# Grouping the bf16 and the float32r products of a split matmul on TensorE

## The chip, the cores and the metric

The kernel runs on one core of a Trainium2 chip. Times are device microseconds (us) of a whole execution. Most executions of one kernel agree within 0.3%; all timed runs used below are in the fast state or, where a kernel was run once, of unknown state with a granted TensorE clock of 0.99 or more. A run that was made once carries a time with an uncertainty of some 0.2%, so for small effects I read the trace, in which one repeated stretch of work is the same to the nanosecond.

## The reference, cut to what matters

```python
def reference(x, w_qkv):            # x: 16 x 512 x 768, w_qkv: 768 x 2304, float32
    qkv = np.matmul(x, w_qkv)
    ...                             # the three column thirds q, k, v, stacked
```

It is one matmul of 8192 rows by 768 by 2304, whose columns are handed out in three parts.

## The kernel before

The kernel multiplies most of the matrix by a Strassen-like scheme with seven products instead of eight. A *pair* is one block of 256 rows; for each pair there are two *quads*, a and b, one for each set of 1024 columns, and 256 remaining columns that are multiplied directly (`rem`). Products 1 and 2 of a quad use the rounded input in bf16. Products 3 to 7 use sums and differences of blocks, in float32r. One product is three matmuls of 512 columns.

```python
    def product(u, n, ps, start):
        t1, t2, t3, t4 = ts[u.q]
        if n <= 2:                                   # bf16
            h = (n - 1) * KH
            lhs = [xb[u.p][:, h + j, :P] for j in range(KH)]
            rhs = [b1[u.q][:, h + j, :] for j in range(KH)]
        else:                                        # float32r
            k, t = {3: (4, b22[u.q][:]), 4: (0, t4), 5: (1, t1), 6: (2, t2), 7: (3, t3)}[n]
            lhs = [sr[u.p][:, k, j, :] for j in range(KH)]
            rhs = [t[:, j, :] for j in range(KH)]
        for j in range(KH):                          # KH = 3
            nc.tensor.matmul(ps[:], lhs[j], rhs[j], ...)

    def do(u, n):
        ...
        if n == 1:
            u.x = bank()
            product(u, 1, u.x, True)
            nc.scalar.activation(c11, u.x[:], ident)
        elif n == 6:                                 # adds to what product 1 left in the bank
            product(u, 6, u.x, False)
            nc.scalar.activation(c12, u.x[:], ident)
        ...                                          # 7 and 4 go on in the same bank in the same way

    def two(a, b, early):                            # one pair; 28 of the 29 pairs of the main part
        do(a, 1)
        do(b, 1)
        early()                                      # transpose, rounding, sums of the next pair
        do(a, 2)
        do(a, 6)
        do(b, 2)
        do(b, 6)
        do(a, 5)
        do(a, 7)
        do(b, 5)
        do(b, 7)
        do(a, 4)
        rem(a.p)                                     # 12 bf16 matmuls of 256 columns
        do(b, 4)
        do(a, 3)
        store_quad(a)
        do(b, 3)
        store_quad(b)
```

The first three row blocks are multiplied directly, and the last pair has its own code, with the same order and early stores.

Of the kernel before, what the change touches and what calls it, by code (L numbers as in the profile page):

```python
# [10 lines left out]
def kernel(  # L11
# [125 lines left out]
    def copy_halves(dst, src, two):  # L137

        nc.vector.tensor_copy(out=dst[0], in_=src[0])  # L139
        if two:  # L140
            nc.scalar.activation(dst[1], src[1], ident)  # L141
        else:
            nc.vector.tensor_copy(out=dst[1], in_=src[1])
# [3 lines left out]
    def cast_rows(p, two=True):  # L147
        src = xin.pop(p)
        xc[p] = s_pool.tile([P, 2, K], bf16, name="xc", tag="s")
        for r in range(2):  # L150
            halves = (slice(0, K // 2), slice(K // 2, K))
            copy_halves([xc[p][:, r, n] for n in halves], [src[:, r, n] for n in halves], two)
# [42 lines left out]
    def product(u, n, ps, start):  # L195
        t1, t2, t3, t4 = ts[u.q]
        if n <= 2:
# [3 lines that stand above are left out]
        else:  # L201
# [3 lines that stand above are left out]
        for j in range(KH):  # L205
            nc.tensor.matmul(  # L206
                ps[:], lhs[j], rhs[j],
                start=(start and j == 0), stop=(j == KH - 1), skip_group_check=True,
            )

    def bank():
        return ps_pool.tile([P, CB], fp32, name="ps")

    def do(u, n):
        c11, c12 = u.o[:, 0, :CB], u.o[:, 0, CB:]
        c21, c22 = u.o[:, 1, :CB], u.o[:, 1, CB:]
# [4 lines that stand above are left out]
        elif n == 2:  # L221
            u.z = bank()
            product(u, 2, u.z, True)
            nc.vector.tensor_tensor(c11, c11, u.z[:], op=add)  # L224
        elif n == 6:
            product(u, 6, u.x, False)
            nc.scalar.activation(c12, u.x[:], ident)  # L227
        elif n == 5:
            u.y = bank()
            product(u, 5, u.y, True)  # L230
        elif n == 7:
            product(u, 7, u.x, False)
            nc.scalar.activation(c22, u.x[:], ident)  # L233
            nc.vector.tensor_tensor(c22, c22, u.y[:], op=add)  # L234
        elif n == 4:
            product(u, 4, u.x, False)
            nc.scalar.activation(c21, u.x[:], ident)  # L237
        elif n == 3:
            product(u, 3, u.y, False)
            nc.vector.tensor_tensor(c12, c12, u.y[:], op=add)  # L240

    def rows_of(s, p, lo, hi):
        return out_flat[s, p * 2 * P:(p + 1) * 2 * P, lo:hi].rearrange("(r m) n -> m r n", m=P)

    def store_quad(u):
        if u.q == 0:
            nc.sync.dma_start(rows_of(0, u.p, 0, H), u.o[:, :, :H])
            nc.sync.dma_start(rows_of(1, u.p, 0, 2 * CB - H), u.o[:, :, H:])
        else:
            part = 2 * H - Q_OFF[1]  # L250
            nc.sync.dma_start(rows_of(1, u.p, H - part, H), u.o[:, :, :part])
            nc.sync.dma_start(rows_of(2, u.p, 0, H), u.o[:, :, part:])

    def rem_row(p, r, ps):
        for j in range(KT):
            nc.tensor.matmul(  # L256
                ps, xb[p][:, j, r * P:(r + 1) * P], w_rem[:, j, :],
                start=(j == 0), stop=(j == KT - 1), skip_group_check=True,
            )

    def rem(p):
        ps = ps_pool.tile([P, 2, REM], fp32, name="ps")
        for r in range(2):
            rem_row(p, r, ps[:, r, :])
        o = or_pool.tile([P, 2, REM], fp32, name="orem")
        nc.scalar.activation(o[:], ps[:], ident)  # L266
        nc.sync.dma_start(rows_of(1, p, R_OFF - H, R_OFF - H + REM), o[:])

    def two(a, b, early):

        do(a, 1)
        do(b, 1)
        early()
        do(a, 2)
        do(a, 6)
        do(b, 2)
        do(b, 6)
        do(a, 5)
        do(a, 7)
        do(b, 5)  # L280
        do(b, 7)
        do(a, 4)
        rem(a.p)
        do(b, 4)
        do(a, 3)
        store_quad(a)
        do(b, 3)
        store_quad(b)

# [164 lines left out]
    for p in range(NS, NP):  # L454
        def early():
            if p + 1 < NP:
                transpose(p + 1)
                round_x(p + 1)
                sums_x(p + 1)
            if p + 2 < NP:  # L460
                load_x(p + 2, nc.scalar)

        if p < NP - 1:
            two(quad(p, 0), quad(p, 1), early)
        else:
            last(quad(p, 0), quad(p, 1))
# [30 lines left out]
```

## Time and profile before

| | before |
|---|---|
| time, median of the first 3 runs | 367.14 us (366.95 to 367.59) |
| TensorE busy, share of the span | 98% |
| one pair, start to start | 10.873 us, the same within 1 ns in all full pairs but the first (10.866) |
| matmuls in a pair | 12 bf16 of 512 columns (B), 12 bf16 of 256 (R), 30 float32r of 512 (F) |
| order in a pair | B9 F3 B3 F18 R12 F9 |

The number to read is not the busy share but the *gap*, the distance from one matmul's start to the next one's. TensorE has work all the time, so the gaps add up to the period of a pair, and 28 of these periods are what the change can move. The lines that show this are in the prediction.

### The profile page before, as it was taken

To read this page: it belongs to the slowest core of one execution; us is meant where nothing else is said; L and a number is where in the kernel's file an instruction comes from. 1 tells how busy PE (TensorE), PEld (TensorE's weight loads), DVE (VectorE), ACT (ScalarE), POOL (GpSimd) and SP (SyncE) were. 2 spreads that over 40 slices of the span, in tenths; PEclk is the share of its full clock that TensorE was granted. 3 is DMA by queue.
4 is the path that set the end of the run, shared out by engine and by line. 5 is a ranking of instruction groups with operands and counts; after the bars stand their busy time and mean duration, and the time that the engine had idled before them with its cause. 6 is when DMAs were issued, how large, how long until landed. Compare 5 with 4: busy or idle time off the path is not lost.

```text
span 364.8 us, 5274 instructions
## 1 busy us (share of the span) xinstructions
PE 358.0 (98%) x1797; PEld 243.8 (67%) x1797; DVE 225.8 (62%) x239; ACT 182.4 (50%) x304; POOL 173.7 (48%) x180
## 2 busy tenths in 40 slices
PE   7999999999999999999999999999999999999995
PEld 3544576666776666776666777676777676777663
DVE  3589746765557665557666556666556766556732
ACT  4557554454454454554455544545545444445442
POOL 0000961655665445665444665444665544566410
PEclk9999999999999999999999999999999999999998
DMA  7999979988899899999888899888899989899767
GB/s 297 382 375 336 347 245 335 327 284 293 273 313 311 264 285 296 277 301 321 278 274 289 281 300 318 284 271 284 288 297 310 296 258 292 291 286 316 261 251 267
DMA packets 80617, 108.08 MB, mean 296 GB/s; under 512 B 4816, under 2 KB 60368, under 8 KB 80592
## 3 DMA queue, kind: packets, MB, share of 16 engines
q1 hardware_dynamic: 65184, 96.35, 80.8%
q10 hardware_dynamic: 15408, 11.41, 9.9%
q8 instruction: 14, 0.23, 0.3%
q14 instruction: 11, 0.09, 0.1%
HBM read 32.24 MB, written 75.50 MB: 295 GB/s over the span
## 4 chain that ended last, share of the span: by engine, by line
PE 97%; DMA 1%; ACT 1%; DVE 0%; issue 0%
PE ps L206 76%; PE ps L256 12%; PE ps L381 9%; DMA xin<-in_x_dram 1%; PE ps L161 1%; ACT xc L141 0%; ACT xb L141 0%; DVE xb L139 0%; ACT orem L311 0%
## 5 line engine op out<-in xcount | busy, mean ns | idle before, releaser
L206 PE MATMUL ps<-t,s 128*128 128x512 f32 x696 | 188.0, 412 | 0.0
L206 PEld LDWEIGHTS ps<-t,s 128*128 128x128 f32 x696 | 128.7, 188 | 30.9
L169 POOL CAST xb<-xf 128x1536 bf16<-128x1536 f32 x29 | 43.9, 1514 | 171.6 <-DVE xf L124 160.1
L124 DVE STREAM_TRANSPOSE xf<-xin 128x1536 f32<-128x1536 f32 x29 | 86.8, 2991 | 6.8 <-DMA xin<-in_x_dram 3.9
L206 PE MATMUL ps<-b,xb 128*128 128x512 bf16 x348 | 85.2, 381 | 0.0
L240 DVE TENSOR_TENSOR o<-o,ps 128x512 f32<-128x512 f32 x58 | 39.9, 688 | 59.3 <-PE ps L206 59.2
L234 DVE TENSOR_TENSOR o<-o,ps 128x512 f32<-128x512 f32 x58 | 39.8, 687 | 54.1 <-ACT o L233 54.1
L206 PEld LDWEIGHTS <-xb 128*128 128x128 bf16 x348 | 29.4, 98 | 42.8 <-issue 14.7
L233 ACT ACTIVATE o<-ps 128x512 f32<-128x512 f32 x58 | 34.8, 600 | 45.2 <-PE ps L206 45.2
L220 ACT ACTIVATE o<-ps 128x512 f32<-128x512 f32 x58 | 34.7, 599 | 43.3 <-DVE o L240 34.6
L227 ACT ACTIVATE o<-ps 128x512 f32<-128x512 f32 x58 | 34.8, 600 | 41.9 <-PE ps L206 41.9
L256 PE MATMUL ps<-w_rem,xb 128*128 128x256 bf16 x384 | 47.5, 273 | 0.0
L206 PE MATMUL ps<-b,s 128*128 128x512 f32 x174 | 44.9, 393 | 0.0
L256 PEld LDWEIGHTS <-xb 128*128 128x128 bf16 x384 | 35.0, 98 | 12.4 <-issue 8.1
L224 DVE TENSOR_TENSOR o<-o,ps 128x512 f32<-128x512 f32 x58 | 36.5, 669 | 2.3 <-ACT o L220 1.3
L206 PEld LDWEIGHTS ps<-b,s 128*128 128x128 f32 x174 | 32.7, 188 | 7.7
L237 ACT ACTIVATE o<-ps 128x512 f32<-128x512 f32 x58 | 34.7, 598 | 4.5 <-ACT orem L311 0.4
L178 POOL TENSOR_TENSOR s<-s,xf 128x384 fp32r<-128x384 f32 x29 | 30.1, 1038 | 2.3
L177 POOL TENSOR_TENSOR s<-xf 128x384 fp32r<-128x384 f32 x29 | 30.9, 1066 | 0.0
L266 ACT ACTIVATE orem<-ps 128x512 f32<-128x512 f32 x31 | 18.6, 599 | 23.5 <-PE ps L256 23.5
L181 POOL TENSOR_TENSOR s<-xf,s 128x384 fp32r<-128x384 f32 x29 | 29.5, 1019 | 0.0
L179 POOL TENSOR_TENSOR s<-xf 128x384 fp32r<-128x384 f32 x29 | 29.2, 1006 | 0.0
(36 smaller groups left out, 128.1 us busy)
## 6 DMA issues: line engine op xcount, KB each, us to landing
out_dram<-o SPq DMA_DIRECT2D x62, 768.0 KB, 5.2
out_dram<-o SPq DMA_DIRECT2D x65, 256.0 KB, 4.8
xin<-in_x_dram SPq DMA_DIRECT2D x62, 192.0 KB, 6.8
xin<-in_x_dram ACTq DMA_DIRECT2D x54, 192.0 KB, 5.6
out_dram<-orem SPq DMA_DIRECT2D x31, 256.0 KB, 2.3
st<-in_w_qkv_dram SPq DMA_DIRECT2D x6, 768.0 KB, 14.1
xin<-in_x_dram SPq DMA_DIRECT2D x3, 768.0 KB, 5.8
st<-in_w_qkv_dram SPq DMA_DIRECT2D x6, 256.0 KB, 6.2
```

The lines of the kernel that those rows point to most:

```text
L124: nc.vector.transpose(t[:].rearrange("p j (g b) -> p g j b", b=G), xin.pop(p)[:].rearrange("p g (a j) -> p g j a", a=G),)
L169: nc.gpsimd.tensor_copy(out=xb[p][:], in_=xf[p][:])
L206: nc.tensor.matmul(ps[:], lhs[j], rhs[j], start=(start and j == 0), stop=(j == KH - 1), skip_group_check=True,)
L220: nc.scalar.activation(c11, u.x[:], ident)
L224: nc.vector.tensor_tensor(c11, c11, u.z[:], op=add)
L227: nc.scalar.activation(c12, u.x[:], ident)
L233: nc.scalar.activation(c22, u.x[:], ident)
L234: nc.vector.tensor_tensor(c22, c22, u.y[:], op=add)
L237: nc.scalar.activation(c21, u.x[:], ident)
L240: nc.vector.tensor_tensor(c12, c12, u.y[:], op=add)
L256: nc.tensor.matmul(ps, xb[p][:, j, r * P:(r + 1) * P], w_rem[:, j, :], start=(j == 0), stop=(j == KT - 1), skip_group_check=True,)
L381: nc.tensor.matmul(ps[n][:], xb[p][:, j, r * P:(r + 1) * P], w[:, j, :], start=(j == 0), stop=(j == KT - 1), skip_group_check=True,)
```

## The change

Its intent: all bf16 work of a pair first (both quads' products and the direct columns), then all float32r products in one run, so that TensorE changes between the two types once per pair instead of three times.

```diff
         do(b, 1)
         early()
         do(a, 2)
+        do(b, 2)
+        rem(a.p)
         do(a, 6)
-        do(b, 2)
         do(b, 6)
         do(a, 5)
         do(a, 7)
         do(b, 5)
         do(b, 7)
         do(a, 4)
-        rem(a.p)
-        do(b, 4)
         do(a, 3)
         store_quad(a)
+        do(b, 4)
         do(b, 3)
         store_quad(b)
```

## The prediction

> **What bounds the kernel now.** I read the page first (busy shares, slices, chain), then the groups of TensorE, then the timeline of one pair's period, then single matmul starts.
>
> The page of the kernel before: shares of the span, the TensorE row and the granted clock in 40 slices, and the chain that ended last.
>
> ```profile
> PE 358.0 (98%) x1797; PEld 243.8 (67%) x1797; DVE 225.8 (62%) x239; ACT 182.4 (50%) x304; POOL 173.7 (48%) x180
> ...
> PE   7999999999999999999999999999999999999995
> ...
> PEclk9999999999999999999999999999999999999998
> ...
> PE 97%; DMA 1%; ACT 1%; DVE 0%; issue 0%
> PE ps L206 76%; PE ps L256 12%; PE ps L381 9%; DMA xin<-in_x_dram 1%; PE ps L161 1%; ACT xc L141 0%; ACT xb L141 0%; DVE xb L139 0%; ACT orem L311 0%
> ```
>
> TensorE is busy in every slice, at full clock, and the chain that ends last is 97% TensorE: 76% the products of the summed pairs (L206), 12% the direct columns (L256). A busy share alone proves little, because matmul ends are modelled, so the proof has to come from starts. From 100 to 340 us the view of waits lists no wait of the matmuls at all; the only wait on a producer for their weights is one of 0.3 us. So time can change only by changing what a matmul costs in its place in the stream, or by making TensorE wait.
>
> The groups of TensorE: matmuls, and weight loads (PEld).
>
> ```profile
> L206 PE MATMUL ps<-t,s 128*128 128x512 f32 x696 | 188.0, 412 | 0.0
> L206 PEld LDWEIGHTS ps<-t,s 128*128 128x128 f32 x696 | 128.7, 188 | 30.9
> ...
> L206 PE MATMUL ps<-b,xb 128*128 128x512 bf16 x348 | 85.2, 381 | 0.0
> ...
> L206 PEld LDWEIGHTS <-xb 128*128 128x128 bf16 x348 | 29.4, 98 | 42.8 <-issue 14.7
> ...
> L256 PE MATMUL ps<-w_rem,xb 128*128 128x256 bf16 x384 | 47.5, 273 | 0.0
> ```
>
> The second number (412, 381, 273 ns) is a latency with overlap; I use the distance between starts instead. The weight loads do differ: 188 ns for float32r, 98 ns for bf16, and both are shorter than the distance between 512-column matmuls (below), so both can hide.
>
> One period (one pair of quads and its remainder columns), TensorE only: start, length, group.
>
> ```profile
> 196.98 2.12 PE L206 MATMUL ps<-b,xb 128*128 128x512 bf16 x9
> 198.74 1.04 PE L206 MATMUL ps<-t,s 128*128 128x512 f32 x3
> 199.63 0.82 PE L206 MATMUL ps<-b,xb 128*128 128x512 bf16 x3
> 200.10 4.50 PE L206 MATMUL ps<-t,s 128*128 128x512 f32 x18
> 204.44 1.49 PE L256 MATMUL ps<-w_rem,xb 128*128 128x256 bf16 x12
> 205.68 0.94 PE L206 MATMUL ps<-t,s 128*128 128x512 f32 x3
> 206.46 1.55 PE L206 MATMUL ps<-b,s 128*128 128x512 f32 x6
> 207.85 1.47 PE L206 MATMUL ps<-b,xb 128*128 128x512 bf16 x6
> ```
>
> The period is 207.85 - 196.98 = 10.87 us (10.873 in the single records, the same to 1 ns in all the full periods) and holds 12 bf16 (B), 12 half-width bf16 (R) and 30 float32r matmuls (F), in the runs B9 F3 B3 F18 R12 F9. There are three entries into float32r and three exits. A reader who divides the groups' starts is misled: B3 seems to take 200.10 - 199.63 = 0.47 us, F18 4.34. The reason is that the first F after a bf16 matmul is recorded early:
>
> ```profile
> 199.85 0.59 PE L206 MATMUL ps<-b,xb 128*128 128x512 bf16 x2
> ...
> 200.10 0.58 PE L206 MATMUL ps<-t,s 128*128 128x512 f32 x1
> ...
> 200.52 0.63 PE L206 MATMUL ps<-t,s 128*128 128x512 f32 x2
> ```
>
> From the single records: the last B to the first F is 28 ns, that F to the next 417 ns. Together 445, and a B (216) and an F (230) cost that anyway. **The entry into float32r is free**; only its record is early.
>
> **What the Trainium skill says.** "TensorE: Matmul & The Clock Gate", section "Back-to-back issue gap", gives N/2.4 + 2.5 ns when warm, thus 216 ns for 512 columns and 109 for 256. The trace agrees for bf16: 216 and 109. Float32r costs 226 to 238 ns here (mean 231), which that section does not list. The same page, "Weight-path perf modes", says the fast weight load is on for 128 weights of a type other than FP32; the 98 against 188 ns fit. It names no price on trn2 for changing between the two paths, so that price must come from this trace. "Perfetto Trace Analysis", section "Tensor Engine Instruction", says that matmul ends are estimates; I therefore use starts only. "PSUM — Partial Sum Buffer" (terms, "PSUM bank") gives eight banks; they matter for the waits below.
>
> **The change part by part.** Counts, shapes and operands of all instructions stay. By the order of instructions VectorE, GpSimd and SyncE are the same; on ScalarE the eviction of the direct columns moves ahead of the c12, c22 and c21 evictions; TensorE becomes B12 R12 F30. So three entries and three exits become one of each, in 28 of the 29 pairs (the last pair has its own code).
>
> 1. Entries, B to F (445 against 446) and R to F (28 + 314 = 342 against 109 + 231 = 340): 0 to 2 ns each. Nothing to gain.
> 2. Exits. The first B after F takes 226 ns instead of 216 (+10), twice per period; the first R after F takes 120 instead of 109 (+11), once. After the change one +10 is left: saves 10 + 11 = 21 ns per period. B to R costs nothing: where the blocks of the head go from bf16 products to direct columns the starts are 216 and then 109 to 110 ns apart.
> 3. Float32r runs. Counting the first F as (gap before it + its own gap - the normal gap of its predecessor), the run of 3 takes 698 ns, of 9 2093, of 18 4151: 232.7, 232.6 and 230.6 ns each. A line of about 230 ns per F plus 9 ns per run gives those within 14 ns. Two runs fewer would save some 20 to 30 ns per period. This is softer: the gaps follow a repeated pattern of 227, 231 and 235 ns, the same in every period, with no correlation to what the other engines do, so I choose 24 ns and allow -40 to +70.
>
> Sum: 21 + 24 = 45 ns per period, 0.4% of 10.87 us; times 28 = 1.3 us. Prediction 367.14 - 1.3 = **365.9 us**. If the intent was that each change of type drains the array, the trace says it does so for 10 ns, not for a matmul.
>
> **The rivals.**
>
> *A new wait on PSUM or on an eviction.* The F run puts all accumulating products close together: a6, b6, a5, a7, b5, b7, a4, a3, b4, b3, of 0.69 us each. Product 7 of a quad must wait for the eviction of c12 after product 6, product 4 for that of c22 after product 7; between them lie two products (1.39 us) in each case. An eviction now starts 0.2 to 0.3 us after its last matmul's start + 0.23 (product 6 of b ends about 200.8 and its c12 eviction starts 201.18) and takes 0.60, so 0.8 to 1.0 us: 0.4 to 0.6 us of slack each. Before, a6 to a7 had three products and a7 to a4 two, so the tight case is not new. ScalarE has 0.60 x 9 = 5.4 us of work in 10.87, and the direct columns' eviction (0.60) now falls at the head of the F run, ahead of a6's, which ends 0.69 us later: no queue. A pair opens seven banks and eight rotate; with the new order the shortest reuse runs from the c21 eviction of b, after b4, to the product 2 of a in the next pair, with three products (2 us) between. This would cost up to some 0.5 us per pair (10 to 14 us) if I have the order wrong; I hold it unlikely, 1%.
>
> *VectorE or GpSimd late.* The transpose (2.97 us) still starts when the c12 addition of b is over, about 0.9 us into the period, and GpSimd's last sum ends at 206.74, 1.1 us before the period's end. The sums are then needed after B12 R12 (3.9 us into the next period) instead of after B9 (1.8), and the rounded x at the same time as before. The change relaxes this.
>
> *Transfers.* DMA share is 0.91 at 290 GB/s from 100 to 340 us, not far from full, but bytes per period are the same; the direct columns are stored 3 us earlier and a's quad one product earlier. No load is needed sooner. If anything the tail, which is untouched code, keeps its length.
>
> *Larger gain.* If float32r settled at its best gap, 227 ns, in a long run (the second half of F18 has five such in a row), 30 x 4.4 = 132 ns per period more, 3.7 us in all: about 363.2 us, still within 2%. If the pattern settled at 235, it would be 3.2 us slower on that term. Against both: F18 already mixes all three gaps.
>
> **Range and chances.** The exits alone give -0.6 us, the float32r term -2.0 to +1.1 us around it, and the three runs of before spread over 0.64 us: 364.6 to 367.1. A 2% change would be 7.3 us, 260 ns per period: more than every switch together costs now (about 45 to 50 ns). Only an unseen wait could do that (slower), or a price of mixing hidden in all 30 float32r gaps (faster): 231 down to 222, below any gap seen in F18. Hence 0.01 faster, 0.98 same, 0.01 slower.
>
> **What would show it.** In the profile after: a period of about 10.83 us, in the order bf16 x12, direct x12, f32 x30; one 226 ns gap and no 120 ns gap left; bf16 gaps still 216 and 109; mean float32r gap 229 to 232; again no wait of the matmuls in the steady part. Wrong if TensorE shows waits on ScalarE or VectorE within the F run, if the float32r mean leaves 228 to 234 ns, or if the first R after a B costs more than 109.

## The result, and the profile after

| | before | after |
|---|---|---|
| time, median of 6 runs each | 367.04 us (366.92 to 367.59) | 366.98 us (366.81 to 367.72) |
| ratio of the fast runs | | 1.0001, 95% interval 0.9988 to 1.0013 |
| one pair, start to start | 10.873 us | 10.887 us |
| sum of the 30 float32r gaps of a pair | 6.942 us | 6.976 us |
| sum of the 24 bf16 gaps of a pair | 3.931 us | 3.910 us |

A ratio here is the mean time of one kernel's fast runs over that of the other's in the same rounds, so it is not quite the ratio of the medians. The time is inside the predicted range, 1.1 us above the predicted point. The interval allows a saving of 0.44 us at most (0.9988), so the predicted saving of 1.3 us did not come. The sums of the table come from the single records of the trace, with the first F of a run counted as in the prediction. The rest of the period is bf16.

The page of the kernel after: shares, the TensorE row and the clock row in 40 slices, the chain that ended last.

```profile
PE 356.6 (98%) x1765; PEld 248.2 (68%) x1797; DVE 224.5 (61%) x239; ACT 182.6 (50%) x304; POOL 173.8 (48%) x180
...
PE   8999999999999999999999999999999999999995
...
PEclk9999999999999999999999999999999999999999
...
PE 96%; ACT 1%; issue 1%; ACTq 0%; DVE 0%
```

TensorE bounds as before. The count 1765 instead of 1797 is a trap: work has not gone away. The weight loads (PEld) are still 1797, and the records of 32 matmuls are missing, mostly that of the first B after each float32r run.

One pair of the kernel after, TensorE only: start, length, group.

```profile
197.29 2.54 PE L206 MATMUL ps<-b,xb 128*128 128x512 bf16 x11
199.66 1.47 PE L256 MATMUL ps<-w_rem,xb 128*128 128x256 bf16 x12
200.89 5.13 PE L206 MATMUL ps<-t,s 128*128 128x512 f32 x21
205.86 0.86 PE L206 MATMUL ps<-b,s 128*128 128x512 f32 x3
206.56 0.85 PE L206 MATMUL ps<-t,s 128*128 128x512 f32 x3
207.26 0.85 PE L206 MATMUL ps<-b,s 128*128 128x512 f32 x3
208.18 2.54 PE L206 MATMUL ps<-b,xb 128*128 128x512 bf16 x11
```

The order is B12 (one record missing) R12 F30, and the pair takes 208.18 - 197.29 = 10.89 us. The last float32r products start 206.56 - 205.86 = 0.70 us apart, 233 ns per matmul. From 100 to 340 us the view of waits again lists no matmul that waited, and only this for the weight loads:

```profile
PEld L206 <- issue: 5.9, 22, 0.3
```

That is the load for the first B of each pair, which is not fetched ahead while float32r runs; before, the same row stood at 11.7 us in 43 times, with 6.0 us more for the direct columns. So the switches are fewer, as meant, and no matmul waits. Yet the pair is 13 ns longer.

Those loads also say what the 10 ns of an exit go with. In the head of the kernel before, where all matmuls are bf16, the first load of the direct columns waited for VectorE:

```profile
13.95 1.09 PEld L256 LDWEIGHTS <-xb 128*128 128x128 bf16 x11 [0.35 <-DVE w_rem L423]
```

The first matmul behind it takes 119 ns to the next start instead of 109, and the first B behind a late load at 17.53 us takes 226, without any change of type. The kernel with no float32r at all (below) also has such a 120, once, at 14.01 us. So the 10 ns also stand behind a late weight load where no type changes; in the steady part loads come late only behind float32r. No run takes the two apart.

The single records say where the time went. Before, two B after F took 226 ns instead of 216 and the first R after F took 120 instead of 109. After, one 226 is left (its record is missing; last F and first B together span 454 ns), B to R costs 109 like any other R, and what the entry from R to F costs is counted with the F. The bf16 part is worth 21 ns, as predicted. The 30 float32r matmuls, each of them the same size on the same kind of data, cost 34 ns *more* than before.

The steady gaps of the run of 30, from the single records, in order, in ns (not a view of the profile):

```
350 234 233 233 231 227 234 235 231 235 232 235 230 236 228 233 231 226
234 235 232 235 232 235 230 236 228 232 235, then the last one and the first B: 454
```

(350 is 28 + 322, from the last R to the second F; 109 of it belong to R.) Before, the run of 18 held a stretch of 230 227 227 226 227 227 ns, in products 5 and 7 of b. In the run of 30 that stretch is gone. The first and the third pair of the changed kernel do still have it: they took 10.840 us (from direct columns to direct columns), close to the predicted 10.83. Already their first F differs, 29 + 314 ns against 28 + 322, after the same direct columns. Then, in the same instruction order, the kernel settles into the pattern above, at 10.886 to 10.887 us, in every pair from the fourth on. (The second pair took 11.000 us: one weight load there waited 0.3 us for GpSimd, once, in the start-up.)

### The profile page after: what moved, and what is told of

Read it like the earlier page. It is cut to its first block, busy times and chain, and to the rows that moved or that the text cites. A ratio compares the mean times of both kernels' runs of the same rounds, so it can differ in the third digit from the quotient of the medians.

```text
span 365.0 us, 5220 instructions
## 1 busy us (share of the span) xinstructions
PE 356.6 (98%) x1765; PEld 248.2 (68%) x1797; DVE 224.5 (61%) x239; ACT 182.6 (50%) x304; POOL 173.8 (48%) x180
## 4 chain that ended last, share of the span: by engine, by line
PE 96%; ACT 1%; issue 1%; ACTq 0%; DVE 0%
PE ps L206 75%; PE ps L256 11%; PE ps L381 9%; PE ps L361 1%; PE ps L161 1%; ACT o L237 0%; ACTq L297 0%; ACT xb L141 0%; ACT orem L311 0%; DVE xb L139 0%; ACT xc L141 0%; ACTq L313 0%; DVE zero L340 0%; ACTq L311 0%
## 5 line engine op out<-in xcount | busy, mean ns | idle before, releaser
L206 PE MATMUL ps<-t,s 128*128 128x512 f32 x696 | 174.0, 398 | 0.0
L124 DVE STREAM_TRANSPOSE xf<-xin 128x1536 f32<-128x1536 f32 x29 | 85.5, 2949 | 6.1 <-DMA xin<-in_x_dram 3.2
L206 PE MATMUL ps<-b,xb 128*128 128x512 bf16 x320 | 74.1, 379 | 1.9
L206 PEld LDWEIGHTS <-xb 128*128 128x128 bf16 x348 | 31.7, 98 | 41.7 <-issue 7.8
L206 PE MATMUL ps<-b,s 128*128 128x512 f32 x174 | 49.7, 395 | 0.0
L256 PEld LDWEIGHTS <-xb 128*128 128x128 bf16 x384 | 37.3, 98 | 11.4 <-issue 0.5
```

The source lines that it names most:

```text
L124: nc.vector.transpose(t[:].rearrange("p j (g b) -> p g j b", b=G), xin.pop(p)[:].rearrange("p g (a j) -> p g j a", a=G),)
L206: nc.tensor.matmul(ps[:], lhs[j], rhs[j], start=(start and j == 0), stop=(j == KH - 1), skip_group_check=True,)
L256: nc.tensor.matmul(ps, xb[p][:, j, r * P:(r + 1) * P], w_rem[:, j, :], start=(j == 0), stop=(j == KT - 1), skip_group_check=True,)
```

## The experiments

What had to be told apart. **My theory** after the result: the exits from float32r cost what I said, and the rest is a property of the float32r stream, whose mean gap depends on the order of the products. **Rivals**: a wait hidden in the long run; a real cost of changing type that is much larger; weight loads as the bound; memory contention. The diffs are against the changed kernel, except for the eight switches and the bf16 sums in the old order, which are against the kernel before.

### One part alone: the products

The changed kernel with `rem` back in its old place: B12 F21 R12 F9.

```diff
-        rem(a.p)
         ...
         do(a, 4)
+        rem(a.p)
+        do(b, 4)
         do(a, 3)
         store_quad(a)
-        do(b, 4)
```

> Only the bf16 products are grouped; the direct columns stay after product 4 of a. Runs per period: B12 F21 R12 F9. Theory S (each exit from float32r costs 10 to 11 ns, the float32r gap does not depend on the order): exits 2 instead of 3, one 226 ns gap and one 120 ns gap per period, period 10.873 - 0.010 = 10.863 us. Theory P (the float32r gap, 227 to 235 ns, depends on where in the stream a product stands, and that is what ate the gain): the exits fall by 10 ns too, but the mean float32r gap leaves 231.4 ns by up to 1.5 ns either way, and the period lies anywhere from 10.82 to 10.91 us. Rival W (a wait appeared in the long float32r run): some gap over 250 ns in each steady period.

Measured: 10.893 us per pair, 20 ns longer than before; 367.4 us in one run. One 226 and one 120 ns gap are there, so the exits fell by 10 ns, and the float32r gaps sum to 6.972 us, 30 ns more. No gap over 250 ns beyond those where a run of F begins, which hold the gap of two. The theory that only the exits matter (10.863 us) is 30 ns off. It falls. Two starts of the first B, one pair apart (208.04 - 197.15 = 10.89 us), and the run of 21 between them:

```profile
197.15 2.76 PE L206 MATMUL ps<-b,xb 128*128 128x512 bf16 x12
199.56 5.22 PE L206 MATMUL ps<-t,s 128*128 128x512 f32 x21
208.04 2.76 PE L206 MATMUL ps<-b,xb 128*128 128x512 bf16 x12
```

### The other part alone: the direct columns

`rem` moved up, product 2 of b left after product 6 of a: B9 R12 F3 B3 F27.

```diff
         do(a, 2)
-        do(b, 2)
         rem(a.p)
         do(a, 6)
+        do(b, 2)
         do(b, 6)
```

> Only the direct columns are moved up, the bf16 products stay split. Runs per period: B9 R12 F3 B3 F27. Theory S: exits 2 (both float32r to bf16 product, +10 each), no 120 ns gap, period 10.873 - 0.011 = 10.862 us. Theory P: the same 11 ns in the bf16 gaps, and a float32r mean that differs from 231.4 ns by up to 1.5 either way (period 10.82 to 10.91 us). Rival W: a gap over 250 ns in each steady period.

Measured: 10.872 and 10.894 us in turn, pair by pair, mean 10.883; 367.39 us in one run. No 120 ns gap; exits of 9 to 14 ns. The float32r gaps sum to about 6.961 us, 19 ns more than before. Neither part alone brings a gain; each loses more in the float32r gaps than it saves at the exits. That one order gives two periods in turn may mean that the pattern depends on the pair before. A rival is not excluded here: the sums (the float32r weights) lie in two buffers that also take turns.

### The opposite: eight switches

The types alternate as often as the dependences allow, with `rem` cut into four parts (`next(rs)` emits three of its 12 matmuls).

```diff
+        do(a, 1); do(a, 5); do(b, 1); early(); do(b, 5)
+        do(a, 2); do(a, 6); do(b, 2); do(b, 6)
+        next(rs); do(a, 7); next(rs); do(b, 7)
+        next(rs); do(a, 4); next(rs); do(b, 4)
+        do(a, 3); store_quad(a); do(b, 3); store_quad(b)
```

> The opposite of the change: bf16 products, direct columns (cut in four) and float32r products alternate, eight exits per period instead of three (four to bf16 products, four to direct columns). Theory S: 4 x 10 + 4 x 11 = 84 ns of exits instead of 31, so the period is 10.873 + 0.053 = 10.926 us, and the time 367.0 + 1.5 = 368.5 us. Theory P adds a float32r term of up to 45 ns per period either way: 10.88 to 10.97 us, 367.2 to 369.8 us. Rival D (the thought behind the change, that each switch of type empties the array for about a matmul, 150 to 230 ns): five more switches cost 0.75 to 1.15 us per period and 21 to 32 us in all, over 385 us. No part of the result depends on the order, so the outputs stay right.

Measured: 371.55 us (4 runs), ratio 1.0119 (1.0102 to 1.0136), 11.040 us per pair. A part of one pair, TensorE only:

```profile
206.28 0.50 PE L274 MATMUL ps<-w_rem,xb 128*128 128x256 bf16 x3
206.53 0.95 PE L206 MATMUL ps<-t,s 128*128 128x512 f32 x3
207.32 0.50 PE L274 MATMUL ps<-w_rem,xb 128*128 128x256 bf16 x3
207.58 0.96 PE L206 MATMUL ps<-t,s 128*128 128x512 f32 x3
208.38 0.50 PE L274 MATMUL ps<-w_rem,xb 128*128 128x256 bf16 x3
```

One R3 F3 group takes 207.32 - 206.28 = 1.04 and 208.38 - 207.32 = 1.06 us, where 3 x 109 + 3 x 231 would be 1.02. So five more switches cost 11.040 - 10.873 = 0.167 us, **33 ns each**. The 33 ns are the whole difference between the kernels: this one also changes the order of the products, and the order alone moves the float32r gaps by some 20 ns and more per pair (below). The idea that a switch costs a whole matmul (over 385 us) is off by far. But the period lies above both of my ranges too. The exits sum to 88 ns where I had said 84, which is right, while the float32r gaps sum to 7.053 us, 111 ns more than before. In runs of three, the last F takes 237 to 240 ns, and between direct columns the other two take 234 to 240 as well, at or above the longest gaps of a long run (235, 236). In this kernel the price lies more in the F next to a switch than in the bf16 matmul after it.

### No float32r at all

The tiles of sums and differences become bfloat16, in the new order and in the old.

```diff
-    f32r = mybir.dt.float32r
+    f32r = mybir.dt.bfloat16
```

> The order of the changed kernel, but the tiles that were float32r are bfloat16, so there is only one type and one weight path (the result loses accuracy on purpose). If the 15 ns by which a float32r gap exceeds a bf16 gap belong to the type and its weight load (188 ns), all 54 gaps become 216 and 109 ns and the period 42 x 216 + 12 x 109 = 10.38 us; 29 periods x 0.5 = 14.5 us less, about 352.5 us. If something else than the type (a wait, reads of VectorE or GpSimd on the same memory) holds the gaps at 231, the period stays near 10.87 us.

> The order of the kernel before, all products in bfloat16 (less accurate on purpose): the fourth corner beside before (10.873 us), after (10.887) and the bfloat16 kernel in the new order (10.375, 352.98 us). If the order acts only through the change of type, then with one type it does nothing: 10.374 to 10.376 us, 352.5 to 353.5 us, no 226 or 120 ns gap. If the new order carries a cost of its own that has nothing to do with types (waits, evictions close together), this one is faster than 10.375 us.

| | float32r sums | bf16 sums |
|---|---|---|
| old order | 10.873 us per pair, 367.04 us | 10.375 us, 352.74 us, ratio 0.9611 (0.9595 to 0.9627) |
| new order | 10.887 us per pair, 366.98 us | 10.375 us, 352.98 us, ratio 0.9618 (0.9603 to 0.9632) |

Groups of TensorE in the old order with bf16 sums, from 200 to 310 us:

```profile
L206 PE MATMUL ps<-t,s 128*128 128x512 bf16 x245 | 59.7, 379 | 0.5
L206 PE MATMUL ps<-b,xb 128*128 128x512 bf16 x132 | 32.1, 379 | 0.0
```

Former float32r matmuls and bf16 matmuls now read alike (379 ns latency), and in the trace the gaps are 216 and 109 ns (give or take the rounding), one after the other, in both orders in the steady part. So the order acts through the type alone, and the new order has no wait of its own. The type costs 0.50 us per pair (0.47 in the 30 gaps, 15.6 ns each, and 0.03 at the exits) and 14 us in all: more than ten times any switch effect in the changed kernel. Both bf16 kernels beat both kernels of this study by 3.8 to 3.9%. They are less accurate: worked out in numpy for 256 rows and 1024 columns, not on the chip, the relative error of the scheme is about 0.006 with bf16 sums against 0.002 with sums kept in float32. Whether that is allowed is a question of the user's, not of the profile.

### Are the weight loads the bound?

A float32r weight load takes 188 ns, a bf16 one 98. Half the columns streamed in products 3, 4, 6 and 7 (wrong result).

```diff
-                ps[:], lhs[j], rhs[j],
+                ps[:, :w], lhs[j], rhs[j][:, :w],      # w = 256 for n in (3, 4, 6, 7), else 512
```

> The changed kernel, but the float32r products 3, 4, 6 and 7 stream 256 columns instead of 512 (wrong result on purpose); product 5 keeps 512. Theory L (a float32r gap is set by its weight load of 188 ns plus a turnaround of some 40 ns, not by the columns streamed): the half-wide gaps stay at 226 to 240 ns and the period near 10.87 us. Rival C (set by the columns): the half-wide gaps fall to 110 to 130 ns and the period by 24 x 0.11 = 2.6 us to about 8.3 us, unless another engine then sets it.

Measured: half-wide float32r gaps of 115 to 121 ns inside a run; 324.17 us in one run. Its TensorE matmuls, and below its weight loads, both from 150 to 280 us:

```profile
L207 PE MATMUL ps<-t,s 128*128 128x256 f32 x252 | 41.1, 290 | 0.0
...
L207 PE MATMUL ps<-b,s 128*128 128x256 f32 x84 | 15.9, 298 | 10.1 <-DVE o L235 10.0
```

```profile
L207 PEld LDWEIGHTS ps<-t,s 128*128 128x128 f32 x336 | 46.5, 189 | 6.3 <-issue 3.7
```

The theory that weight loads set the gap falls: the loads still take 189 ns each, longer than the gap, so they overlap one another, and the gap follows the columns. Per column float32r costs 7 to 8% more than bf16 at either width: 231 against 216, and about 118 against 109. The kernel does not reach 8.3 us per pair, because TensorE now waits for VectorE (10.0 us in the row above) and for GpSimd; the expectation had named that possibility.

### Are there hidden waits?

The evictions between the products of a quad read a tile of zeros instead of the bank (wrong result), so the products no longer wait for them.

```diff
-            nc.scalar.activation(c12, u.x[:], ident)
+            nc.scalar.activation(c12, zero[:], ident)      # likewise c11 and c22, and the addition to c22
```

> The changed kernel, but the evictions after products 1, 6 and 7 and the addition of product 5 read a zero tile instead of the bank (wrong result on purpose), so TensorE has no wait on ScalarE or VectorE between the products of a quad; number and size of the evictions stay. Theory H1 (the pattern of 227 to 235 ns comes from the waits, or the wait instructions, among the float32r products): the pattern changes, most gaps become equal, the period leaves 10.887 us. Rival H2 (it comes from the float32r stream itself): the same gaps in the same order within 2 ns, period 10.88 to 10.89 us. Theory W (hidden waits cost time): period falls by more than 50 ns.

Measured: 10.886 to 10.887 us per pair, and the same 30 gaps in the same order within 1 ns. In one run it took 368.16 us. The waits on these evictions, and the instructions that carry them, have no part in the pattern. The run also speaks against memory contention from these engines: ScalarE's and VectorE's work on c22 moved 1.2 us or more earlier in the pair, and the gaps stayed. Transfers and GpSimd were not moved. This run also has the record of the first B that the changed kernel lacks: the last F takes 228 ns, and that B and the next 442 together, 226 + 216.

### Do the operands decide the pattern?

First, every float32r product reads one and the same set of operands (wrong result).

```diff
-            k, t = {3: (4, b22[u.q][:]), 4: (0, t4), 5: (1, t1), 6: (2, t2), 7: (3, t3)}[n]
+            k, t = 0, ts[0][0]
```

> The changed kernel, but every float32r product reads the same three weight slices and the same three moving slices (wrong result on purpose). Theory A (a gap depends on where the operands lie): the gaps repeat with a cycle of three and the pattern of 12 or 13 matmuls is gone. Rival H2 (the stream has a pattern of its own): the cycle of 12 to 13 gaps between 226 and 236 ns stays, and the period is 10.84 to 10.89 us.

Measured: 10.920 us per pair, 368.37 us in one run; the gaps alternate 232, 235, 232, 235 through the whole run, with no gap below 231. The cycle of 12 or 13 is gone, so operands matter; but the cycle is two, not three, so no theory as put was right.

Then the half of it: own sums as weights, one streamed tile for all.

```diff
+        if n > 2:
+            rhs = [ts[0][0][:, j, :] for j in range(KH)]
```

> The changed kernel, but every float32r product streams the same three slices of one weight-difference tile, while its own input sums stay (wrong result on purpose): the half of the one-operand-pair run that is left apart. Theory M (the streamed operand decides the gap pattern): the even alternation of 232 and 235 ns of that run appears and the period is 10.92 us. Rival S2 (the loaded sums decide it, or only both together): the cycle of 12 to 13 gaps between 226 and 236 ns stays, 10.88 to 10.89 us.

Measured: 10.920 us and the same alternation of 232 and 235; 367.86 us in one run. All 30 records are there:

```profile
201.44 7.25 PE L208 MATMUL ps<-t,s 128*128 128x512 f32 x30
208.53 2.76 PE L208 MATMUL ps<-b,xb 128*128 128x512 bf16 x12
```

So the *streamed* operand changes the pattern, and with one streamed tile it does not show which weights are loaded. Whether it is the streamed tile's place, its values, or the change from tile to tile was not taken apart. And the rows confirm the sum without any missing record: 208.53 - 201.44 = 7.09 us, less the 0.08 by which the first F is recorded early, 7.01 us for 30, 233.7 ns each.

Last, does it matter where the weights lie? The buffers of the sums are moved by 256 bytes, and by 12 kB.

```diff
+    pad_pool = ctx.enter_context(tc.tile_pool(name="pad", bufs=1))   # ahead of s_pool, 256 bytes
```

```diff
+    s_pool = ctx.enter_context(tc.tile_pool(name="s", bufs=2))       # now ahead of xb_pool
     xb_pool = ctx.enter_context(tc.tile_pool(name="xb", bufs=4))
```

> The changed kernel with 256 bytes per partition put ahead of the buffers of the input sums, so that these (the weights of the float32r products) lie 256 bytes further; order, waits and counts are the same. If the gap pattern depends on the place of the operands in fine steps, it changes and the period leaves 10.887 us by more than 3 ns; if not, the same gaps and 10.886 to 10.887 us.

> The changed kernel with the buffers of the input sums allocated before those of the rounded input, thus 12 kB per partition lower; order, waits and counts are the same. If the gap pattern depends on the place of the operands in coarse steps, the period leaves 10.887 us by more than 3 ns; if it does not depend on place, the same gaps and 10.886 to 10.887 us.

Measured: 10.886 to 10.887 us in both from the fourth pair on, the same gaps in the same order; 367.16 and 367.0 us in one run each. These two moves of the weights change nothing in the settled pattern. (The first three pairs do differ, 10.870 to 10.883 us in the first and third, so the way into the settled pattern depends on small things.)

### Another order in the same run

```diff
         do(a, 6)
-        do(b, 6)
         do(a, 5)
+        do(b, 6)
         do(a, 7)
```

> The changed kernel with another order inside the float32r run: 6a 5a 6b 7a 5b 7b 4a 3a 4b 3b instead of 6a 6b 5a 7a 5b 7b 4a 3a 4b 3b. Same number of exits (one). Theory S (only the exits matter): 10.887 us to within 3 ns. Theory P (the mean float32r gap depends on the order): the exits stay as they are (one 226 ns gap), but the mean float32r gap is another than 232.5 ns, somewhere in 230.5 to 233.5, and the period in 10.83 to 10.92 us.

Measured: 10.867 us per pair; 366.55 us in one run, beside 367.28 for the kernel before. Two starts one pair apart, each of the second B (as in the kernel after, the record of the first is missing):

```profile
197.31 2.54 PE L206 MATMUL ps<-b,xb 128*128 128x512 bf16 x11
208.17 2.54 PE L206 MATMUL ps<-b,xb 128*128 128x512 bf16 x11
```

Same switches, same waits, same exit (455 ns for the last F and the first B), but the float32r gaps sum to 6.957 us, 19 ns less than in the changed kernel, and the stretch of 226 to 227 ns is back in products 5 and 7 of b. One swap of two products is worth as much as the two exits that the change removed. 20 ns in 28 pairs is 0.6 us, though, which one run cannot show in the time, so this is a finding about gaps, not a faster kernel.

The float32r term across the runs that have 30 of 512 columns per pair:

| run | float32r runs per pair | sum of F gaps | mean F |
|---|---|---|---|
| before | 3, 18, 9 | 6.942 us | 231.4 ns |
| after, settled | 30 | 6.976 | 232.5 |
| after, first and third pair | 30 | 6.930 | 231.0 |
| products only | 21, 9 | 6.972 | 232.4 |
| direct columns only | 3, 27 | 6.961 (mean of two) | 232.0 |
| other order | 30 | 6.957 | 231.9 |
| one streamed tile | 30 | 7.010 | 233.7 |
| eight switches | seven of 3 and one of 9 | 7.053 | 235.1 |

## Why the prediction was right or wrong

The verdict, no change beyond 2%, was right, and 366.98 us lies in the range. The point was 1.1 us too low, 0.3%. One term, number 4 below, was 58 ns per pair off, 1.6 us in 28 pairs. That the time still fell in the range, 0.1 us below its top, is partly luck: the pairs alone became 0.39 us longer, which on 367.14 us would lie outside, and the rest of the run and the spread of the runs went the other way.

1. *TensorE bounds, and only gaps or waits can move the time*: right. The share stays at 98%, the chain at 96%, no matmul waits in the steady part, and removing the waits on evictions left every gap as it was within 1 ns.
2. *Entries are free*: nearly. In the changed kernel the first F after R costs 28 + 322 - 109 = 241 ns, 9 more than the mean and 8 more than before (28 + 314 - 109 = 233); with eight switches it is 229 to 238. This cost is counted with the F.
3. *Exits save 21 ns per pair*: right, 3.931 to 3.910 us in the bf16 gaps. B to R is free, as read from the head of the old trace.
4. *Float32r runs save 24 ns per pair*: **this step failed.** I drew a line through three runs and read "9 ns per run" out of it (which gives 18 ns for two runs fewer, not the 24 that I chose). Measured is +34 instead of -24, inside the -40 to +70 that I allowed (as a saving) but with the other sign, and the mean of 232.5 ns is outside the 229 to 232 that I named as the sign. The line had taken a stretch of short gaps in the run of 18 for an effect of length. With one run of 30 the sum was 6.930, 6.957, 6.976 or 7.010 us, by the order, the streamed tile and the pair. Length shows only at the short end, where the kernel with seven runs of three costs more; its order differs too.
5. *Sum*: -21 + 34 = +13 ns, and 10.873 became 10.887. Over the pairs from the first to the last pair's start the changed kernel takes 0.39 us longer, of which about 0.11 us is the second pair. That is below what the runs can tell apart, hence 1.0001.
6. *Rivals*: no wait on eviction or bank; GpSimd late once, by 0.3 us; no matmul waited for a transfer. The large gain (all gaps at 227) did not come. The prediction named the idea of a whole array drained per switch as not in the trace; eight switches confirmed it, at 33 ns each. Its remark that the gaps have "no correlation" to the other engines proved nothing, since in a steady trace everything repeats with the same period; the run without eviction waits is the test.
7. *Two slips of sum*, which change nothing in the call: its own terms reach 367.7 us where the range ends at 367.1, and the larger gain comes to 367.14 - 0.6 - 3.7 = 362.8 us, not 363.2.

What stays open: why the gap of a float32r matmul moves between 226 and 236 ns with the tile that is streamed, and why one instruction order has a pair of 10.840 and one of 10.887 us. Shown is that it is not the waits on evictions, not the two moves of the weights, not the length of the weight load; the streamed tiles were not moved. One clue lies in the traces: averaged over 20 pairs, the settled periods (10866.65, 10873.30, 10886.65, 10893.30, 10919.95 and 11039.95 ns) are multiples of 6.667 ns (1630, 1631, 1633, 1634, 1638, 1656) to within 0.05 ns; of "direct columns only" two pairs together are (21766.6 ns, 3265). The bf16 kernels are not (10375.00 ns, 1556.25). So the float32r stream seems to fall into step with something of this pitch; no run tests that.

## What to carry to other kernels

Before reordering work to save switches, read from the trace what a switch costs, as gaps between starts on both sides of it: here 10 ns at an exit, 33 ns with nearly everything in runs of three, never a whole matmul. Where two removed switches are worth 0.2% of a period, a change of a few ns in each of 30 matmuls outweighs them, and three points on a line do not predict that change. The large term was in plain sight: what one float32r matmul costs over a bf16 one, times all of them, was 3.8% and more than any order could bring.

## What the Trainium skill lacked or had wrong

- "TensorE: Matmul & The Clock Gate", section "Back-to-back issue gap": it has no figure for float32r. Here 512 columns take 226 to 240 ns in the settled pairs, mean 231 to 235 by kernel, and 256 columns about 118, while bf16 takes 216 and 109. The section also calls about 131 ns the sustained spacing for 512 columns in a stream of loads and matmuls; here a long run of bf16 matmuls stays at 215 to 216 ns, each with its own load.
- The same page, section "Weight-path perf modes": no price for changing between bf16 and float32r. Here it is 10 to 14 ns on the bf16 matmul after float32r, and about 33 ns per switch when nearly all runs are three long. The same 10 ns stand without a change of type behind a late weight load (119 for 109 ns, 226 for 216).
- No page has it: the gap of a float32r matmul depends on the streamed tile (alternating 232 and 235 ns with one tile, 226 to 236 ns with the kernel's own), and the same order of instructions took 10.840 us in two early pairs and 10.887 us in the settled ones.
